# Inverse softmax sums as transposed rows, their transfers and the sum stores in ScalarE's stream, and the x norm in parts

## The chip, the cores and the metric

The kernel runs on one core of one Trainium2 chip. A core has five instruction streams, each worked off strictly in its order: PE (TensorE, matmuls), DVE (VectorE), ACT (ScalarE), POOL (GpSimd) and SP (SyncE, which here only issues transfers). A stream that waits for a semaphore holds everything behind it. A transfer (DMA) is issued by one of SP, ACT or POOL and runs on 16 DMA engines that all of them share; whoever needs its data waits for its semaphore. The metric is the device time of one execution in microseconds.

## The reference

One decoder block for 512 tokens of width 1024, in float32. The input is RMS-normed and projected to q, k, v and a gate z for two attention branches of 8 heads of 64, to two sigmoid gates, and to 8 forget logits:

```python
h = rms_norm(x, norm_g[layer])
proj = h @ w_in[layer]
fq, fk, fv, fz, mq, mk, mv, mz, ga, gb, fl = split_cols(proj, IN_SPLITS)
q = rms_norm(to_heads(fq, FOX_HEADS), fox_q_g[layer]); k = ...; v = to_heads(fv, FOX_HEADS)
log_f = log_sigmoid(fl + b_f[layer])
y_fox = from_heads(fox_attention(q, k, v, log_f)) * silu(fz)     # causal softmax with decay
q = partial_rope(rms_norm(to_heads(mq, MOBA_HEADS), moba_q_g[layer]), positions); k = ...
y_moba = from_heads(moba_attention(q, k, v)) * silu(mz)
merged = (sigmoid(ga + b_gate[layer, 0]) * (y_fox @ w_fox[layer])
          + sigmoid(gb + b_gate[layer, 1]) * (y_moba @ w_moba[layer]))
x = x + merged @ w_out[layer]
```

With 512 tokens and blocks of 256, the block-sparse branch selects every earlier block, so both branches are full causal softmax attention. Each softmax row is divided by its sum; this change is about how the inverses of these sums get to where they are used.

## The kernel before, in words

Tokens are cut into 4 tiles of 128, the width into 8 chunks `k` of 128. A float32 product is made of three matmuls with operands split into a high and a low part (`h`, `l`); `split` makes these parts for each weight chunk, on ACT and DVE. Weights come in pieces of 512 KB over SP's queue (`wr`).

The program is written as a list of units, but a planner orders each engine's stream by its own estimate of a timeline. So the order of the source is a wish; the stream order is what the planner made of it. Dependencies become semaphore waits in those streams.

The stages:

- Head. The first q and k projections run on unnormed input (`Z`, with the gain folded in). `x_stats` gives the inverse norm `r` per token. `normalise` broadcasts `r` over partitions (four PE transposes into `p_rbc`, a copy to `rbc`) and scales the eight chunks `XT[k]`, each one product on DVE, one copy to `Gh` on ACT, one subtraction to `Gl` on DVE. The gate units `fza` and `fzb` (`unit_z`, two each) multiply `Z` with weights, scale by `rbc` (`zs`) and apply SiLU. `forget` computes the log-sigmoid of the forget logits in about 30 small DVE operations and one exponential, its cumulated sum by matmul, and `LR` through `p_LR`.
- Attention, in four groups of four heads: fox a, fox b, moba a, moba b. In a group, `Tr(pr)` transposes q and k of a pair of heads (`p_qT`, `p_kT`); `Aa(h)` makes logits (`lg`), the masked maximum on DVE, the exponential with row sums `rsum` on ACT (L521); `Bb(h)` transposes the probabilities (`p_a`, `p_b`, `p_cc`), splits them (`pth`, `ptl`) and multiplies with v (`pv`); `Yp(pr)` multiplies the pair's output with z and the inverse sums and splits it (`yh`, `yl`). Between these pieces stand the projections of the next group as filler (`pj`): each evacuated unit of q or k goes through `norm_qk` (square on ACT, sum `ss` on DVE, power `ff` and product `qn` on POOL, L301 and L303) and, for moba, `do_rope` on POOL (L333 to L339). `Tr` of the next group waits for these `qn`.
- The inverse sums. After the second head of a pair, `inverse_sums` takes the reciprocal `ri` (`rinv`) of 128 partitions by 8 values, writes it to DRAM from POOL's queue as `r_dram` (L535), and reads each head's 512 values back, spread over 64 partitions, into `rinv_bc` (L537, two loads, also POOL's queue). `Yp` multiplies z into `rinv_bc` on POOL (L593; on DVE for the last pair) and DVE multiplies the result into `ypair` (L594).
- The activation sums. `make_sums(k)` forms four sums and differences of chunks of the normed input for the gates' fast block product, splits them, and stores them from POOL's queue to DRAM (L242, 16 stores of 256 KB); `load_sums` reads them at the start of the gates.
- Gates and output: block products `GA`, `GB`, the branch projections `wf`, `wm`, and `wo` with the residual.

PSUM has the pools `pj` (2 buffers), `tp` (3), `lg` (2) and `pv` (1). In `attn_group` three lists are returned: head, body and tail of a group; the main part interleaves body and tail with filler and the next group's head.

Of the kernel before, what the change touches and what calls it, by code (L numbers as in the profile page):

```python
# [29 lines left out]
def fox_moba_kernel(ctx: ExitStack, tc, xT, x, w_in, w_fl, w_fox, w_moba, w_out, cst, rope, out):  # L30
# [37 lines left out]
    def col(c, n=1):  # L68
        return cs[:, c:c + n]
# [137 lines left out]

    rbc = con.tile([P, S], F32, name="rbc")

    def normalise():  # L210

        p = pst("lg", 2, "p_rbc")
        for t in range(NT):
            T.transpose(p[:, t * P:(t + 1) * P], r[:, t:t + 1].to_broadcast([P, P]), ident)
        A.activation(rbc, p, AF.Copy)
        for k in range(KT):
            V.scalar_tensor_tensor(XT[k], XT[k], col(C_NG + k), rbc, op0=OP.mult, op1=OP.mult)
            A.activation(Gh[:, k, :], XT[k], AF.Copy)
            V.tensor_tensor(out=Gl[:, k, :], in0=XT[k], in1=Gh[:, k, :].bitcast(F32), op=OP.subtract)
# [8 lines left out]
    def make_sums(k):  # L228
        def tl(tag, dt=F32):
            return t2("y", 15, f"sum_{tag}", dt=dt)  # L230
        a, b = XT[k], XT[k + 4]
        f0, f1 = tl("sf"), tl("sf")
        s3, s2, s1, s4 = f0[:, 0:HT], f0[:, HT:S], f1[:, 0:HT], f1[:, HT:S]
        for o, x, y, op in ((s3, a[:, 0:HT], a[:, HT:S], OP.subtract), (s1, a[:, HT:S], b[:, HT:S], OP.add),
                            (s2, s1, a[:, 0:HT], OP.subtract), (s4, b[:, 0:HT], s2, OP.subtract)):
            V.tensor_tensor(out=o, in0=x, in1=y, op=op)
        for i, f in enumerate((f0, f1)):
            hl = [tl("sh", F32R), tl("sl", F32R)]
            A.activation(hl[0], f, AF.Copy)
            V.tensor_tensor(out=hl[1], in0=f, in1=hl[0].bitcast(F32), op=OP.subtract)  # L240
            for d, t in zip(S_dram, hl):
                nc.gpsimd.dma_start(out=d[2 * i:2 * i + 2, :, k, :].rearrange("s p t -> p s t"),  # L242
                                    in_=t.bitcast(F32).rearrange("p (s t) -> p s t", t=HT))

    def load_sums():
        for i in range(4):
# [130 lines left out]

    def unit_z(name, c):
        def go():
            p = pj(f"pz_{name}{c}")  # L380
            tr_mm(p, name, c)
            z = t2("y", 15, f"zs_{name}{c}")
            s = t2("u", 4, "sg")
            if name[0] == "f":
                V.tensor_tensor(out=z, in0=p, in1=rbc, op=OP.mult)
                A.activation(s, z, AF.Sigmoid)
                V.tensor_tensor(out=z, in0=z, in1=s, op=OP.mult)
            else:
# [10 lines left out]
    def zero_kl():  # L399
# [6 lines left out]
        for o in range(2):  # L406
            rows = slice(HD, P) if o == 0 else slice(0, HD)
            for tl in KLt[o] + [Q2t[o]]:
                G.memset(tl[rows, :].bitcast(F32), 0.0)

    def forget():
        n = NT * 8
        f2 = xf.rearrange("p t h -> p (t h)")

        def sm(nm, w=n):
            return stage["pool"].tile([P, w], F32, name=nm)
        na, e, d, s, s2, acc, lf = (sm(f"fg_{i}") for i in range(7))
        pre = stage["pool"].tile([P, NT, 8], F32, name="fg_pre")
        V.tensor_scalar(na, f2, -1.0, None, op0=OP.mult)
        V.tensor_tensor(out=na, in0=na, in1=f2, op=OP.min)  # L420
        A.activation(e, na, AF.Exp)
# [48 lines left out]
    def attn_group(br, half, gq, gk):  # L470
# [36 lines left out]
        def Aa(h):  # L507
            def go():
                qs, kh, kl, q2 = st[h]
                hh = hb + h  # L510
                pts = []
                for i in range(NT):
                    n = P * (i + 1)
                    lg = pst("lg", 2, "lg")
                    qt = slice(i * P, (i + 1) * P)
                    T.matmul(lg[:, :n], qs[:, qt], kh[:, :n], start=True, stop=False)  # L516
                    T.matmul(lg[:, :n], q2[:, qt], kl[:, :n], start=False, stop=True)  # L517
                    pt = stage["pool"].tile([P, n], F32, name=f"p{i}", tag=f"p{i}", bufs=2)
                    V.tensor_tensor_reduce(pt, lg[:, :n], mask[:, 512 - n:512], -0.125, 3.0e38,  # L519
                                           op0=OP.add, op1=OP.min, accum_out=mkn[:, hh, i:i + 1])  # L520
                    A.activation(pt, pt, AF.Exp, bias=mkn[:, hh, i:i + 1], scale=-1.0,  # L521
                                 accum_out=rs[:, hh, i:i + 1])
                    pts.append(pt)
                st[h] = pts
                if h % 2:
                    inverse_sums(h // 2)
            return go

        def inverse_sums(pr):


            h0 = hb + 2 * pr
            V.reciprocal(ri[:, h0:h0 + 2, :], rs[:, h0:h0 + 2, :])
            rb = st["r", pr] = stage["pool"].tile([P, S], F32, name="rinv_bc", tag="rinv_bc", bufs=1)
            G.dma_start(out=R_dram[h0:h0 + 2].rearrange("h t p -> p h t"), in_=ri[:, h0:h0 + 2, :])  # L535
            for o in range(2):
                G.dma_start(out=rb[o * HD:(o + 1) * HD, :],  # L537
                            in_=R_dram[h0 + o].rearrange("t p -> (t p)").partition_broadcast(HD))

        def Bb(h):  # L540
            def go():
# [39 lines left out]
                sh = t2("u", 4, "ysh")  # L581
                A.activation(sh[me, :], pv[ot, :], AF.Copy)  # L582
                V.tensor_tensor(out=y[me, :], in0=pv[me, :], in1=sh[me, :], op=OP.add)  # L583
            return go

        def Yp(pr):
# [10 lines left out]
                Y[br, gp] = (yh, yl)  # L597
            return go

        return ([Tr(0)], [Aa(0), Aa(1), Tr(1), Bb(0), Aa(2), Bb(1), Yp(0), Aa(3)], [Bb(2), Bb(3), Yp(1)])  # L600


    FS, MG = {}, {}
# [247 lines left out]
        evac_qk(b1[t], "fqa", t)  # L851
    for t in range(NT):
        evac_qk(b2[t], "fka", t)
    normalise()
    pump(0)
    fz = filler(["fza", "fzb"])
    for u in fz[:2]:
        u()
    forget()
    for u in fz[2:]:  # L860
        u()
    seq(["fva"])
    enter("attention")
    zero_kl()
# [5 lines left out]
    head, body, tail = attn_group("f", "a", col(C_FQ), col(C_FK))  # L870
    HALF[0] = False
    head[0]()
    for n in range(4):
        nxt = []
# [86 lines left out]
```

## Time and profile before

| what | us |
|---|---|
| median of three runs | 472.12 |
| their range | 471.99 to 472.58 |
| the profiled execution, as a run | 476.4 |
| its span, first to last instruction | 474.7 |
| PE busy | 435.7 (92%) |
| DVE busy | 311.9 (66%) |
| ACT busy | 262.0 (55%) |
| POOL busy | 115.6 (24%) |
| granted PE clock, mean | 0.959 |

All stretches and durations come from the one profiled execution. A row of the waits names engine, tile and line of the waiting instruction and then what ended the wait. A row of a timeline gives start and duration in us, engine, line, operation, what it writes and reads, shapes, and in brackets the idle time of the engine before it. A row of stretches gives the busy time of PE, PE's weight loads, DVE, ACT and POOL, then the granted clock of PE as a share of full speed. Issuing a transfer is not counted as busy on ACT, but is on POOL. Matmuls are pipelined, so neighbouring rows overlap.

### The profile page before, as it was taken

The page shows a single profiled execution, that of the slowest core. Times are in us where ns is not written, and L with a number is a line of the kernel's source. Part 1 is how long each engine was busy: PE and PEld are TensorE (multiplying, and loading weights), DVE is VectorE, ACT ScalarE, POOL GpSimd, SP SyncE. Part 2 cuts the span into 40 slices and gives each one's busy share as a digit, 9 for nine tenths or more (in the row PEclk, how much of TensorE's full clock was granted, in tenths as well). Part 3 has the DMA queues.
Part 4 walks back from the last instruction along what each step waited for, and adds up shares of the span by engine and source line. Part 5 has one row for each costly group of instructions (what it writes and reads, how often), then busy time and mean ns, then how long its engine had stood idle before and what let it go on. Part 6 is the DMA issues. An engine that isn't in the chain of part 4 may idle for free.

```text
span 474.7 us, 8105 instructions
## 1 busy us (share of the span) xinstructions
PE 435.7 (92%) x3092; PEld 408.9 (86%) x3092; DVE 311.9 (66%) x553; ACT 262.0 (55%) x489; POOL 115.6 (24%) x146
## 2 busy tenths in 40 slices
PE   7998999996999939999597989978999999999997
PEld 6996899995999937899596768868999989989996
DVE  5489997686368654578544588634889788664411
ACT  5877456784478633797423588633755645532200
POOL 4046058206338351103563001231000000000000
PEclk9999999998899977999889889997999999999999
DMA  8970478572442712411424130119331611652331
GB/s 257 379 252 11 133 236 269 147 115 58 78 134 46 62 51 63 116 57 26 129 59 110 35 100 0 24 34 402 120 103 76 206 61 62 204 178 83 121 111 44
DMA packets 22390, 56.39 MB, mean 119 GB/s; under 512 B 3472, under 2 KB 7696, under 8 KB 22352
## 3 DMA queue, kind: packets, MB, share of 16 engines
q1 hardware_dynamic: 14240, 39.98, 28.8%
q0 software_dynamic: 3456, 10.52, 7.5%
q10 hardware_dynamic: 4656, 5.38, 4.3%
q8 instruction: 24, 0.39, 0.4%
q14 instruction: 14, 0.11, 0.1%
HBM read 46.27 MB, written 6.32 MB: 111 GB/s over the span
## 4 chain that ended last, share of the span: by engine, by line
PE 58%; DMA 21%; DVE 6%; POOL 6%; ACT 5%; issue 3%; POOLq 0%; DVEq 0%; ACTq 0%
DMA r_dram<-rinv 8%; DMA rinv_bc<-r_dram 6%; PE pb_GB L681 3%; PE pb_GB L684 3%; PE pb_GB L683 3%; PE pb_GA L681 3%; PE pb_GA L684 3%; PE pb_GA L683 3%; PE po L781 2%; PE po L783 2%; PE po L782 2%; POOL ff L301 2%; DMA wr_fka<-in_w_in_dram 2%; DMA x<-in_x_dram 2%; DMA KH<-KH 2%
## 5 line engine op out<-in xcount | busy, mean ns | idle before, releaser
L521 ACT ACTIVATE p<-p,negm 128x128 f32<-128x128 f32 (+1 forms) x64 | 35.6, 557 | 7.5 <-DVE negm L519 7.2
L519 DVE CUSTOM_DVE_ANT_0 p<-lg,mask 128x128 f32<-128x128 f32 (+1 forms) x64 | 30.2, 483 | 13.3 <-PE lg L517 12.8
L301 POOL TENSOR_TENSOR ff<-ss,mh 128x8 f32<-128x8 f32 x16 | 28.7, 1800 | 21.3 <-DVE ss L299 20.6
L781 PE MATMUL po<-wh_wo,mgh 128*128 128x256 f32 x96 | 27.1, 282 | 0.0
L783 PE MATMUL po<-wh_wo,mgl 128*128 128x256 f32 x96 | 27.1, 282 | 0.0
L782 PE MATMUL po<-wl_wo,mgh 128*128 128x256 f32 x96 | 27.0, 281 | 0.0
L537 POOL DMA_DIRECT2D rinv_bc<-r_dram x16 | 8.6, 540 | 65.0 <-DMA r_dram<-rinv 56.0
L791 DVE TENSOR_TENSOR ot<-po,xr 128x256 f32<-128x256 f32 x16 | 6.6, 425 | 24.8 <-PE po L783 23.6
L112 DVE TENSOR_TENSOR wl_GA<-wr_ga,wh_GA 128x1024 fp32r<-128x1024 f32 x14 | 16.9, 1221 | 8.8 <-ACT wh_GA L110 5.8
L516 PE MATMUL lg<-KH,QS 128*128 128x128 f32 (+1 forms) x64 | 21.4, 341 | 0.7 <-DMA KH<-KH 0.4
L494 DVE SCALAR_TENSOR_TENSOR KL<-p_kT,cs,KH 64x512 fp32r<-64x512 f32 x16 | 12.0, 749 | 15.2 <-ACT KH L492 14.8
L110 ACT ACTIVATE wh_wo<-wr_wo 128x1024 fp32r<-128x1024 f32 x8 | 8.5, 1061 | 21.6 <-PE po L783 8.0
L110 ACT ACTIVATE wh_GA<-wr_ga 128x1024 fp32r<-128x1024 f32 x14 | 14.6, 1059 | 10.3 <-PE pb_GA L683 4.4
L582 ACT ACTIVATE ysh<-pv 64x512 f32<-64x512 f32 x16 | 9.5, 594 | 18.3 <-PE pv L558 18.1
L112 DVE TENSOR_TENSOR wl_GB<-wr_gb,wh_GB 128x1024 fp32r<-128x1024 f32 x14 | 16.8, 1222 | 4.2 <-ACT wh_GB L110 3.3
L110 ACT ACTIVATE wh_GB<-wr_gb 128x1024 fp32r<-128x1024 f32 x14 | 14.6, 1058 | 8.5 <-PE pm L611 2.5
L781 PEld LDWEIGHTS po<-wh_wo,mgh 128*128 128x128 f32 x96 | 18.1, 189 | 0.0
L782 PEld LDWEIGHTS po<-wl_wo,mgh 128*128 128x128 f32 x96 | 18.1, 189 | 0.0
L783 PEld LDWEIGHTS po<-wh_wo,mgl 128*128 128x128 f32 x96 | 18.1, 188 | 0.0
L492 ACT ACTIVATE KH<-p_kT,cs 64x512 fp32r<-64x512 f32 x16 | 10.8, 678 | 13.0 <-PE p_kT L482 12.8
L535 POOL DMA_DIRECT2D r_dram<-rinv x8 | 7.7, 957 | 38.1 <-DVE negm L519 33.6
L583 DVE TENSOR_TENSOR ypair<-pv,ysh 64x512 f32<-64x512 f32 x16 | 11.0, 688 | 8.8 <-ACT ysh L582 8.6
(449 smaller groups left out, 1843.8 us busy)
## 6 DMA issues: line engine op xcount, KB each, us to landing
wr_ga<-in_w_in_dram SPq DMA_DIRECT2D x8, 512.0 KB, 4.1
wr_gb<-in_w_in_dram SPq DMA_DIRECT2D x8, 512.0 KB, 5.1
wr_wo<-in_w_out_dram SPq DMA_DIRECT2D x8, 512.0 KB
xt<-in_xT_dram SPq DMA_DIRECT2D x8, 256.0 KB
x<-in_x_dram SPq DMA_DIRECT2D x8, 256.0 KB, 7.7
s_dramh<-sum_sh POOLq DMA_DIRECT2D x8, 256.0 KB, 3.8
s_draml<-sum_sl POOLq DMA_DIRECT2D x8, 256.0 KB, 4.5
KH<-KH ACTq DMA_DIRECT2D x16, 128.0 KB, 3.0
```

The costliest lines, as they stand in the source:

```text
L110: A.activation(hi[:, :, 0:n], src, AF.Copy)
L112: eng.tensor_tensor(out=lo[:, q, 0:n], in0=src[:, q], in1=hi[:, q, 0:n].bitcast(F32), op=OP.subtract)
L301: G.tensor_tensor(out=f2, in0=ss.rearrange("p t h -> p (t h)"), in1=mh, op=OP.pow)
L516: T.matmul(lg[:, :n], qs[:, qt], kh[:, :n], start=True, stop=False)
L519: V.tensor_tensor_reduce(pt, lg[:, :n], mask[:, 512 - n:512], -0.125, 3.0e38, op0=OP.add, op1=OP.min, accum_out=mkn[:, hh, i:i + 1])
L521: A.activation(pt, pt, AF.Exp, bias=mkn[:, hh, i:i + 1], scale=-1.0, accum_out=rs[:, hh, i:i + 1])
L681: T.matmul(o, hi[:, k, cc], lh, start=(n < 3 and c == 0 and k == 0), stop=False, skip_group_check=True)
L683: T.matmul(o, hi[:, k, cc], ll, start=False, stop=False, skip_group_check=True)
L684: T.matmul(o, lo[:, k, cc], lh, start=False, stop=(k == 3), skip_group_check=True)
L781: T.matmul(p[:, :CW], gh[:, st], hi[:, k, :CW], start=(kk == 0), stop=False)
L782: T.matmul(p[:, :CW], gh[:, st], lo[:, k, :CW], start=False, stop=False)
L783: T.matmul(p[:, :CW], gl[:, st], hi[:, k, :CW], start=False, stop=(kk == KT - 1))
```

## The change

Four things change.

The inverse sums. `inverse_sums` keeps only the reciprocal. `sums_out`, at the end of `Bb` of a pair's first head, has PE transpose the 128 by 8 values to 8 by 128 in a `tp` buffer, ACT copy them to `rinv_t`, and ACT's queue store the eight rows to `r_dram`. `sums_in` issues the two loads of `rinv_bc` from ACT's queue: for a group's first pair after `Aa(2)`, for the second after `Bb(3)`.

The sum stores. `make_sums` returns a function that issues its four stores from ACT's queue, called after the unit that follows. The sums move from the units of `fqb` and `fkb` to those of `fvb` and `mqa`.

The head. `norm_row` makes `rbc`; `normalise` takes some of the chunks, and the three parts (0 to 2, 3 to 5, 6 and 7) stand behind the first three gate units. `forget_exp` (the argument and the exponential) comes ahead of it, the rest of `forget` behind all four gate units. `fzb` uses `tp` buffers for its products instead of `pj`.

The gate of a group's second pair. `Yp(1)` leaves the tail; it stands behind the first piece of the next group's body, and in the last group between the two units of `wf3`.

```diff
-    def normalise():
-
+
+    def norm_row():
         p = pst("lg", 2, "p_rbc")
         for t in range(NT):
             T.transpose(p[:, t * P:(t + 1) * P], r[:, t:t + 1].to_broadcast([P, P]), ident)
         A.activation(rbc, p, AF.Copy)
-        for k in range(KT):
+
+    def normalise(*ks):
+        for k in ks:
             V.scalar_tensor_tensor(XT[k], XT[k], col(C_NG + k), rbc, op0=OP.mult, op1=OP.mult)
...
-            for d, t in zip(S_dram, hl):
-                nc.gpsimd.dma_start(out=d[2 * i:2 * i + 2, :, k, :].rearrange("s p t -> p s t"),
-                                    in_=t.bitcast(F32).rearrange("p (s t) -> p s t", t=HT))
+            out.extend((d[2 * i:2 * i + 2, :, k, :].rearrange("s p t -> p s t"),
+                        t.bitcast(F32).rearrange("p (s t) -> p s t", t=HT)) for d, t in zip(S_dram, hl))
+
+        def store():
+            for d, t in out:
+                A.dma_start(out=d, in_=t)
+        return store
...
-            p = pj(f"pz_{name}{c}")
+            p = (tp if name == "fzb" else pj)(f"pz_{name}{c}")
...
+    def forget_exp():
+        f2 = xf.rearrange("p t h -> p (t h)")
+        FG.extend(stage["pool"].tile([P, NT * 8], F32, name=f"fg_{i}") for i in range(7))
+        na, e = FG[:2]
+        V.tensor_scalar(na, f2, -1.0, None, op0=OP.mult)
+        V.tensor_tensor(out=na, in0=na, in1=f2, op=OP.min)
+        A.activation(e, na, AF.Exp)
...
                 if h % 2:
                     inverse_sums(h // 2)
+                elif h:
+                    sums_in(0)
             return go
 
         def inverse_sums(pr):
             h0 = hb + 2 * pr
             V.reciprocal(ri[:, h0:h0 + 2, :], rs[:, h0:h0 + 2, :])
+
+        def sums_out(pr):
+            h0 = hb + 2 * pr
+            p = tp("p_ri")
+            T.transpose(p[:8, :P], ri[:, h0:h0 + 2, :].rearrange("p h t -> p (h t)"), ident)
+            rt = sb.tile([8, P], F32, name="rinv_t", tag="rinv_t", bufs=1)
+            A.activation(rt, p[:8, :P], AF.Copy)
+            A.dma_start(out=R_dram[h0:h0 + 2].rearrange("h t p -> (h t) p"), in_=rt)
+
+        def sums_in(pr):
             rb = st["r", pr] = stage["pool"].tile([P, S], F32, name="rinv_bc", tag="rinv_bc", bufs=1)
-            G.dma_start(out=R_dram[h0:h0 + 2].rearrange("h t p -> p h t"), in_=ri[:, h0:h0 + 2, :])
             for o in range(2):
-                G.dma_start(out=rb[o * HD:(o + 1) * HD, :],
-                            in_=R_dram[h0 + o].rearrange("t p -> (t p)").partition_broadcast(HD))
+                A.dma_start(out=rb[o * HD:(o + 1) * HD, :],
+                            in_=R_dram[hb + 2 * pr + o].rearrange("t p -> (t p)").partition_broadcast(HD))
...
                 V.tensor_tensor(out=y[me, :], in0=pv[me, :], in1=sh[me, :], op=OP.add)
+                if o == 0:
+                    sums_out(pr)
+                elif pr:
+                    sums_in(1)
             return go
...
-        return ([Tr(0)], [Aa(0), Aa(1), Tr(1), Bb(0), Aa(2), Bb(1), Yp(0), Aa(3)], [Bb(2), Bb(3), Yp(1)])
+        return ([Tr(0)], [Aa(0), Aa(1), Tr(1), Bb(0), Aa(2), Bb(1), Yp(0), Aa(3)], [Bb(2), Bb(3)], [Yp(1)])
...
-    normalise()
+    forget_exp()
+    norm_row()
     pump(0)
     fz = filler(["fza", "fzb"])
-    for u in fz[:2]:
+    for k, u in enumerate(fz):
         u()
+        if k < 3:
+            normalise(*range(3 * k, min(3 * k + 3, 8)))
     forget()
-    for u in fz[2:]:
-        u()
...
-                def with_sums(u=fill[2 * k], k=k):
+                store = []
+
+                def with_sums(u=fill[2 * k + 8], k=k, store=store):
                     u()
-                    make_sums(k)
-                fill[2 * k] = with_sums
+                    store.append(make_sums(k))
+
+                def with_store(u=fill[2 * k + 8 + 1], store=store):
+                    u()
+                    store[0]()
+                fill[2 * k + 8], fill[2 * k + 8 + 1] = with_sums, with_store
         inter(body + ([following] if n < 3 else []) + tail, fill)
         if n < 3:
-            body, tail = nxt[1:]
+            body, tail = nxt[1][:1] + gate + nxt[1][1:], nxt[2]
+            gate = nxt[3]
+    wf3 = filler(["wf3"])
+    wf3[0]()
+    gate[0]()
+    wf3[1]()
     enter("gates")
     load_sums()
-    seq(["wf3", "GA0", "GA1", "GB0", "wm0", "wm2", "GB1"])
+    seq(["GA0", "GA1", "GB0", "wm0", "wm2", "GB1"])
```

More of the change, by code (lines that the diff above doesn't have):

```diff
@@ L231, in make_sums @@
         a, b = XT[k], XT[k + 4]
+        out = []
         f0, f1 = tl("sf"), tl("sf")
@@ L409, in zero_kl @@
                 G.memset(tl[rows, :].bitcast(F32), 0.0)
+    FG = []
+    def forget_exp():
[5 more added lines that the diff above has]
+        A.activation(e, na, AF.Exp)
     def forget():
@@ L413, in forget @@
         f2 = xf.rearrange("p t h -> p (t h)")
-        def sm(nm, w=n):
-            return stage["pool"].tile([P, w], F32, name=nm)
-        na, e, d, s, s2, acc, lf = (sm(f"fg_{i}") for i in range(7))
+        na, e, d, s, s2, acc, lf = FG
         pre = stage["pool"].tile([P, NT, 8], F32, name="fg_pre")
-        V.tensor_scalar(na, f2, -1.0, None, op0=OP.mult)
-        V.tensor_tensor(out=na, in0=na, in1=f2, op=OP.min)
-        A.activation(e, na, AF.Exp)
         V.tensor_scalar(d, e, 2.0, None, op0=OP.add)
@@ L869, in fox_moba_kernel @@
             ("m", "b", C_MQ, C_MK, ["mzb", "wf0", "wf1", "wf2"]))
-    head, body, tail = attn_group("f", "a", col(C_FQ), col(C_FK))
-    HALF[0] = False
+    head, body, tail, gate = attn_group("f", "a", col(C_FQ), col(C_FK))
     head[0]()
```

## The prediction

> **What bounds the kernel now.** I read the waits of the matmul engine (PE) first, then what its releasers did in that time, then the granted clock behind each wait. The waits of PE, longest first (engine, line, releaser: total us, times, longest us):
>
> ```profile
> PE p_kT L482 <- POOL qn_mka L339: 8.1, 1, 8.1
> PE p_qT L480 <- POOL qn_mqb L339: 5.6, 1, 5.6
> PE pv L558 <- DVE ptl L554: 4.9, 1, 4.9
> PE p_kT L482 <- POOL qn_mkb L339: 4.6, 1, 4.6
> PE p_kT L482 <- POOL qn_fkb L303: 4.5, 1, 4.5
> PE pz_fzb L372 <- DVE fg L426: 2.3, 1, 2.3
> ```
>
> Four gaps end when POOL has normalised a q or k tile, one when DVE has made `ptl`, one in the head of the kernel. Together they are 30.0 us. The reader is to see that no throughput explains them: each is one long wait. The timeline of POOL shows what it did before (start, duration, instruction, idle time before it and its releaser):
>
> ```profile
> 108.57 1.08 POOL L537 DMA_DIRECT2D rinv_bc<-r_dram  x2 [9.01 <-issue]
> ...
> 164.10 1.09 POOL L537 DMA_DIRECT2D rinv_bc<-r_dram  x2 [6.70 <-DMA r_dram<-rinv]
> ...
> 171.07 1.26 POOL L593 TENSOR_TENSOR rinv_bc<-zs_fzb,rinv_bc 128x512 f32<-128x512 f32 x1 [5.32 <-DMA rinv_bc<-r_dram]
> ...
> 177.91 0.44 POOL L339 TENSOR_TENSOR qn_mka<-ra,rb 128x128 f32<-128x128 f32 x1
> ...
> 224.25 1.09 POOL L537 DMA_DIRECT2D rinv_bc<-r_dram  x2 [8.07 <-DMA r_dram<-rinv]
> ...
> 253.14 1.10 POOL L537 DMA_DIRECT2D rinv_bc<-r_dram  x2 [7.31 <-DMA r_dram<-rinv]
> ```
>
> POOL stands still for 6.7 to 9.0 us until the inverse sums have landed in DRAM, issues the two loads that spread them over partitions, and stands still again until these land (5.32 us at 171.07). Only then it goes on to `qn_mka`, whose last step ends at 178.35, where the 8.1 us gap ends. The fifth gap is the same chain on DVE, which does the multiplication L593 of the last pair itself, with `ptl` behind it in its stream:
>
> ```profile
> 321.22 0.69 DVE L593 TENSOR_TENSOR rinv_bc<-zs_mzb,rinv_bc 128x512 f32<-128x512 f32 x1 [8.49 <-DMA rinv_bc<-r_dram]
> ```
>
> A gap costs more than its length. Stretches with busy times and, after POOL, the granted clock: first the work right behind the five long gaps, then the short gap in the head.
>
> ```profile
> 117.51:121.90 4.39, 4.39 (x21) 4.39 (x22) 1.51 (x3) 1.82 (x3) 3.96 (x3) 0.50 0.46 120
> 178.40:183.30 4.90, 4.90 (x19) 4.51 (x20) 2.88 (x4) 3.78 (x6) 0.87 (x1) 0.50 0.49 125
> 237.90:241.30 3.40, 3.39 (x16) 3.39 (x17) 2.58 (x4) 1.99 (x5) 3.32 (x2) 0.50 0.41 117
> 262.14:265.20 3.06, 3.06 (x9) 2.49 (x10) 1.55 (x3) 2.05 (x3) 0.00 (x0) 0.50 0.15 33
> 322.60:326.70 4.10, 4.10 (x19) 4.10 (x20) 2.44 (x3) 0.80 (x2) 0.00 (x0) 0.50 1.02 410
> ```
> ```profile
> 42.00:44.30 2.30, 0.01 (x2) 0.04 (x1) 2.30 (x5) 2.15 (x4) 1.00 (x1) 1.00 0.00 0
> ```
>
> After each long gap PE works 3.1 to 4.9 us at a granted clock of 0.50, 19.85 us together. At full clock that is half the time: 9.9 us lost beside the gaps. So 27.7 (five gaps) + 9.9 + 2.3 = 39.9 us hang on the waits that this change touches. In the 246 us of attention the engines stand thus:
>
> ```profile
> 80.00:326.00 246.00, 215.74 (x1455) 199.57 (x1454) 157.39 (x318) 151.06 (x318) 81.50 (x99) 0.93 0.35 82
> ```
>
> PE is busy 216, DVE 157, ACT 151, POOL 82 us: ACT, which takes the transfers over, has 95 us free, and 61 if some 34 us go from the stretch.
>
> **The change part by part.** What lands how fast (KB each, median us from issue to landing), and what ACT's and PE's pieces cost:
>
> ```profile
> KH<-KH ACTq DMA_DIRECT2D x16, 128.0 KB, 3.0
> rinv_bc<-r_dram POOLq DMA_DIRECT2D x16, 128.0 KB, 5.3
> ...
> out_dram<-ot ACTq DMA_DIRECT2D x16, 128.0 KB, 2.3
> ...
> r_dram<-rinv POOLq DMA_DIRECT2D x8, 4.0 KB, 9.5
> ```
> ```profile
> L521 ACT ACTIVATE p<-p,negm 128x128 f32<-128x128 f32 (+1 forms) x64 | 35.6, 557 | 7.5 <-DVE negm L519 7.2
> L110 ACT ACTIVATE wh_GA<-wr_ga 128x1024 fp32r<-128x1024 f32 x14 | 14.6, 1059 | 10.3 <-PE pb_GA L683 4.4 <-PE pf L611 3.1 <-issue 2.8
> L553 ACT ACTIVATE pth<-p_a 128x512 fp32r<-128x512 f32 x16 | 9.5, 593 | 4.1 <-PE p_a L547 4.0
> L521 ACT ACT_TABLE_LOAD x4 | 5.1, 1283 | 0.1
> ```
> ```profile
> 76.27 0.60 PE L454 MATMUL p_LR<-ident,c 128*64 128x128 f32 x4
> 76.71 0.60 PE L480 MATMUL p_qT<-ident,qn_fqa 128*128 128x128 f32 x4
> 77.15 0.60 PE L482 MATMUL p_kT<-ident,qn_fka 128*128 128x128 f32 x4
> ```
>
> Rows instead of single values: `r_dram<-rinv` moves 4 KB as 1024 separate floats and takes 9.5 us. After the change it is eight rows of 128 floats from ACT's queue. The trace has no such small row transfer; the nearest row is `out_dram<-ot`, also ACT's queue into DRAM, 2.3 us at 128 KB. Ends: 2.3, and 9.5 if it is the write to DRAM and not the form that costs. I take 2.3 to 3.0 (`KH<-KH`, same queue). Added ahead of it are the PE transpose, a copy and a hand-over, under 1 us. The chain to the multiplication is then shorter by 9.5 − 3.5 = 6.0 us.
>
> POOL's stream: all 8 stores and 16 loads of the inverse sums and the 16 stores of the activation sums leave it. POOL keeps its wait for `rinv_bc`, ahead of the q and k norms as before. Take 6.0 us off each gap: 8.1 leaves 2.1; 5.6, 4.6, 4.5 and 4.9 leave nothing. The order of the streams is planned anew, and in the changed order POOL has the whole `mkb` chain behind one such wait, so I leave 3.0 of 27.7 (ends 0 and 12, half of each gap but the largest, rounded up): −24.7.
>
> The clock: with one gap of 2 to 3 us left instead of five over 4.4, I leave 1.0 of 9.9 (end: 4): −8.9. [...]
>
> Norm in parts: `fzb` takes its accumulators from another pool (`tp`, three buffers) and no longer waits for DVE, which had eight `xt` products and eight `Gl` subtractions ahead. DVE's total stays, and the log-sigmoid chain moves behind the gate units; its user, `p_LR`, comes at 76 us. −2.0 of 2.3 (ends 0 and −2.3).
>
> PE: eight more transposes; four of `p_qT` take 77.15 − 76.71 = 0.44 us of its stream, so 8 × 0.11 = +0.9. They borrow a `tp` buffer until ACT has copied it; cover is the other two.
>
> ACT gets 40 more DMA issues. One takes 0.47 us, but in the sequencer, while the engine still works off what it had:
>
> ```profile
> 87.97 0.67 ACT L492 ACTIVATE KH<-p_kT,cs 64x512 fp32r<-64x512 f32 x1
> 88.14 0.47 ACTq L503 DMA_DIRECT2D Q<-QS  x1
> 88.54 0.61 ACT L521 ACTIVATE p<-p,negm 128x384 f32<-128x384 f32 x1
> ```
>
> That is 18.8 us of issue, mostly covered. Eight small copies, at most 0.4 each: 3. In the changed order the gate's sigmoids of the last group stand apart: two more table loads, 2.6. And a new wait: the first load of each pair waits in ACT's stream until the store has landed, and every softmax exponential, PSUM copy and weight split queues behind it. In the changed order the instructions between store and load are, by the durations above: one of 0.6 us (four pairs), 1.5 (one pair), and 2.2 to 2.7 (three pairs), 11.1 us in all. With a landing of 2.3 the uncovered rest is 4 × 1.7 + 0.8 + 0.1 = 7.7 us; with 3.0 it is 12.9. ACT's extra is thus 18.8 + 3 + 2.6 + 7.7 = 32 us against 61 free. PE waits for little of it, since its stream holds projection matmuls that ask nothing of ACT. I charge half of the uncovered waits, +4.0 (ends 0, and 32 if nothing is covered). The sum stores also wait on ACT for DVE's low halves, inside these ends.
>
> Sum against the profiled span: 474.7 − 24.7 − 8.9 − 2.0 + 0.9 + 4.0 = 444.0. That execution took 476.4 as a run, the median of the runs is 472.12, which is 2.6 under its span. Predicted: 444.0 − 2.6 = 441 us, 6.5% faster.
>
> **The rivals.**
>
> ACT binds beside PE. In the changed order 12 of the 16 sum stores stand in ACT's stream within the second group of heads, beside its own work. For: its extra 32 us come in half the span's time and its stream is in order. Against: 61 us free. If half of the 32 reaches PE instead of 4: 441 + 12 = 453 us.
>
> Everything fits: no gap left, no charge for ACT (−3 −1 −4): 433 us. For: the planner now orders around transfers that are short. Against: POOL's waits for `rinv_bc`, 5.3 us, stay.
>
> The other side: the store is slow because it writes DRAM, not because of its form. Then ACT instead of POOL stands still, 8 × 9.5 − 11.1 = 65 us. With all of it passed on to PE the sum is 441 − 4 + 65 = 502 us. It decides from a landing L where 8L − 11.1 exceeds the gain without ACT's charge, 35 us: L = 5.8 us, for all eight pairs. Against: 2.3 us of `out_dram`, with 32 times the bytes. [...]
>
> The change does not do what it says: the new plan puts the q and k chains as late again relative to PE, with POOL's own work (from the end of L593 at 172.33 to `qn_mka` at 178.35 a norm and rope chain takes 6.0 us) as the bound. Then gaps of the old size stay, less the clock and the head: about 470 us, equal within 0.5%.
>
> **How the numbers follow.** Forecast, 434 to 450 (ends: residual gaps 0 to 5, ACT 0 to 8): 0.60. ACT beside PE, 450 to 462: 0.18. Everything fits, under 434: 0.13. ACT blocked, over 473: 0.06. Plan as late as before: 0.03, split between the three signs. The range that leaves out about 2 in 10 is 430 to 459. Faster by over 0.2% (about what a measurement of this kernel can tell from no change) 0.92, same 0.01, slower 0.07.
>
> **What would show it.** Right: POOL has no wait for `r_dram`; its landing is under 3.5 us; the waits of PE on `qn` tiles are under 3 us each; clock 0.98 or more over the span; ACT shows waits of 1 to 2 us at the loads of `rinv_bc`. Wrong: `r_dram` landing above 5 us, or ACT idle before PSUM copies with PE waiting for ACT; a gap at `p_kT` over 4 us with the clock at 0.50 behind it; the stretch from first to last softmax over 225 us.

## The result, and the profile after

| what | before | after |
|---|---|---|
| median, us (four runs each, one chip) | 472.27 | 444.25 |
| range, us | 471.99 to 472.58 | 442.54 to 445.73 |
| profiled execution as a run, us | 476.4 | 445.57 |
| its span, us | 474.7 | 443.8 |
| granted PE clock, mean | 0.959 | 0.992 |

The ratio is 0.9405, with a 95% interval of 0.9361 to 0.945: 28.0 us less. The forecast was 441, inside a range of 430 to 459.

The busy line of the page after:

```profile
PE 430.1 (97%) x3100; PEld 405.3 (91%) x3100; DVE 310.7 (70%) x553; ACT 266.7 (60%) x499; POOL 88.5 (20%) x106
```

The span fell by 30.9 us. PE's busy time fell by 435.7 − 430.1 = 5.6 and its idle time by the other 25.3. The waits of PE after the change, longest first, without those at the program's start and end:

```profile
PE pb_GA L709 <- ACT e_GA L719: 2.5, 1, 2.5
PE pf L638 <- ACT f L652: 1.7, 2, 1.2
...
PE pv L580 <- ACT pth L576: 1.2, 2, 0.8
PE pv L581 <- DVE ptl L577: 0.6, 1, 0.6
```

No wait on any `qn` tile is left: the four gaps of 4.5 to 8.1 us behind POOL are gone, not merely shorter. Of what is left, the three longest end with ACT. POOL still waits in front of its gate multiplication, for the load of `rinv_bc` (this row counts four of these waits), but no longer for the store of the sums:

```profile
POOL rinv_bc L620 <- DMA rinv_bc<-r_dram: 23.9, 4, 17.0
```

The chain that ended last shows how long a store and a load take now (start, duration, what):

```profile
177.97 2.41 DMA r_dram<-rinv_t
...
289.66 6.55 DMA rinv_bc<-r_dram
```

2.41 us for this store, where the median had been 9.5. But the last load of `rinv_bc` takes 6.55 us, where the median had been 5.3. The timelines of ACT and then of DVE around that load, and a stretch (columns as in the prediction: busy PE, its weight loads, DVE, ACT, POOL, then clock, DMA share, GB/s):

```profile
289.13 0.45 ACTq L560 DMA_DIRECT2D rinv_bc<-r_dram  x1
...
289.66 0.58 ACTq L560 DMA_DIRECT2D rinv_bc<-r_dram  x1
...
298.47 0.63 ACT L622 ACTIVATE yhm<-ypair 128x512 fp32r<-128x512 f32 x1 [6.39 <-DVE ypair L621]
```
```profile
296.30 0.69 DVE L620 TENSOR_TENSOR rinv_bc<-zs_mzb,rinv_bc 128x512 f32<-128x512 f32 x1 [5.29 <-DMA rinv_bc<-r_dram]
```
```profile
289.00:296.30 7.30, 6.25 (x50) 5.91 (x49) 1.57 (x3) 1.39 (x3) 0.91 (x2) 1.00 0.95 297
```

The DMA engines are 95% busy, with the activation sums that the gates read and with weights. DVE waits 5.29 us for `rinv_bc`, ACT 6.39 us for DVE, and the copy `e_GA` that PE needs stands behind it in ACT's stream. That is the 2.5 us gap, now the largest.

The clock. First the two stretches that ran at half clock, then, in the same order, the stretch of 3.41 us ahead of each:

```profile
262.21:265.62 3.41, 3.41 (x10) 2.67 (x9) 3.38 (x9) 1.96 (x7) 0.00 (x0) 0.50 0.18 38
299.75:303.17 3.42, 3.42 (x17) 3.42 (x18) 2.65 (x4) 2.21 (x3) 0.00 (x0) 0.50 0.06 16
258.79:262.21 3.42, 1.77 (x8) 1.14 (x8) 2.49 (x4) 3.34 (x6) 0.00 (x0) 1.00 0.00 0
296.34:299.75 3.41, 0.90 (x8) 0.70 (x7) 2.65 (x4) 1.28 (x3) 0.00 (x0) 1.00 0.06 22
```

Two such stretches are left, 6.8 us of work at half clock or 3.4 us lost. Of those in the profile of before, the first and the fifth of six, with the sum of all six:

```profile
115.08:121.91 6.83, 4.40 (x21) 4.41 (x22) 3.92 (x7) 1.82 (x3) 6.31 (x5) 0.50 0.30 77
...
278.92:282.34 3.42, 3.31 (x13) 2.47 (x11) 3.36 (x12) 3.31 (x9) 0.00 (x0) 0.50 0.05 13
...
sum 37.56, PE 23.40 PEld 21.61 DVE 25.43 ACT 17.01 POOL 20.51; mean PE 3.90 PEld 3.60 DVE 4.24 ACT 2.83 POOL 3.42
```

23.4 us of work at half clock, 11.7 lost. The gain from the clock is thus 11.7 − 3.4 = 8.3 us between these two profiles. In a second profile of the changed kernel, `after_again` below, only the later of the two stretches is at half clock.

### The profile page after: what moved, and what is told of

Same layout as the page of the kernel before. It is cut to its first block, busy times and chain, and to the rows that moved or that the text cites. A ratio compares the mean times of both kernels' runs of the same rounds, so it can differ in the third digit from the quotient of the medians.

```text
span 443.8 us, 8080 instructions
## 1 busy us (share of the span) xinstructions
PE 430.1 (97%) x3100; PEld 405.3 (91%) x3100; DVE 310.7 (70%) x553; ACT 266.7 (60%) x499; POOL 88.5 (20%) x106
## 4 chain that ended last, share of the span: by engine, by line
PE 82%; DVE 6%; DMA 5%; ACT 5%; issue 1%; ACTq 0%; SPq 0%; DVEq 0%
PE pb_GB L709 3%; PE pb_GB L711 3%; PE pb_GB L712 3%; PE pb_GA L709 3%; PE pb_GA L712 3%; PE pb_GA L711 3%; PE po L809 3%; PE po L811 3%; PE po L810 3%; PE pv L581 2%; PE pv L580 2%; PE lg L527 2%; PE lg L528 2%; PE pm L638 2%; PE pm L639 2%; PE pm L640 2%
## 5 line engine op out<-in xcount | busy, mean ns | idle before, releaser
L308 POOL TENSOR_TENSOR ff<-ss,mh 128x8 f32<-128x8 f32 x16 | 27.6, 1726 | 78.6 <-DVE ss L306 76.4
L819 DVE TENSOR_TENSOR ot<-po,xr 128x256 f32<-128x256 f32 x16 | 6.6, 424 | 24.8 <-PE po L811 23.6
L501 DVE SCALAR_TENSOR_TENSOR QS<-p_qT,cs,QS 64x512 fp32r<-64x512 f32 x16 | 12.0, 750 | 7.1 <-ACT QS L500 6.7
L577 DVE TENSOR_TENSOR ptl<-p_a,pth 128x512 fp32r<-128x512 f32 x16 | 11.0, 688 | 5.9 <-ACT pth L576 5.8
L638 PE MATMUL pf<-yhf,wh_wf 128*128 128x512 f32 x32 | 13.4, 419 | 1.7 <-ACT f L652 1.7
L112 DVE TENSOR_TENSOR wl_wo<-wr_wo,wh_wo 128x1024 fp32r<-128x1024 f32 x8 | 9.8, 1222 | 7.4 <-ACT wh_wo L110 7.4
```

Of the source, the lines that this page charges most:

```text
L112: eng.tensor_tensor(out=lo[:, q, 0:n], in0=src[:, q], in1=hi[:, q, 0:n].bitcast(F32), op=OP.subtract)
L308: G.tensor_tensor(out=f2, in0=ss.rearrange("p t h -> p (t h)"), in1=mh, op=OP.pow)
```

## The experiments

The runs fall into three groups, each on a chip of its own. The kernel before took 476.69, 473.46 and 477.18 us in them, so times are compared within a group.

**First group: form or queue?** The theory: the store was slow because it wrote 1024 single floats, and rows cure that wherever they are issued. The first rival: it is ScalarE's queue that helps.

`rows_pool`, the changed kernel with the row store and its loads from GpSimd's queue:

```diff
-            A.dma_start(out=R_dram[h0:h0 + 2].rearrange("h t p -> (h t) p"), in_=rt)
+            G.dma_start(out=R_dram[h0:h0 + 2].rearrange("h t p -> (h t) p"), in_=rt)
...
-                A.dma_start(out=rb[o * HD:(o + 1) * HD, :],
+                G.dma_start(out=rb[o * HD:(o + 1) * HD, :],
```

> The changed kernel with the row store and the two loads of the inverse sums issued from POOL's queue again; transpose, copy and everything else as changed. Theory 'form': what cost was the landing of 1024 single floats, 9.5 us, whichever stream waits for it. Then POOL waits 2 to 3 us per pair where it waited 7 to 9, no wait of PE on a qn tile is over 3 us, and the time is 442 to 450 us. Rival 'queue': what cures is that POOL's stream has no wait between store and load at all. Then the q and k norms are late again, PE waits 4 us and more for qn tiles with the clock at 0.50 behind them, and the time is 455 to 470 us.

Measured: 442.44 us, ratio 0.9255 (0.919 to 0.9319). Landing of the transfers, then POOL's waits:

```profile
rinv_bc<-r_dram POOLq DMA_DIRECT2D x16, 128.0 KB, 3.2
...
r_dram<-rinv_t POOLq DMA_DIRECT2D x8, 4.0 KB, 2.3
```
```profile
POOL rinv_bc L620 <- DMA rinv_bc<-r_dram: 13.4, 5, 4.5
POOL rinv_bc L560 <- DMA r_dram<-rinv_t: 11.5, 6, 3.4
```

From the same queue that had needed 9.5 us, the rows land in 2.3. POOL waits again for store and load, 1.9 and 2.7 us on average and 4.5 at most, and PE waits for no `qn` tile. So the form did it, in this order of streams.

`before_rows`, the other way round: the kernel before, with the transpose alone.

```diff
-            G.dma_start(out=R_dram[h0:h0 + 2].rearrange("h t p -> p h t"), in_=ri[:, h0:h0 + 2, :])
+            p = tp("p_ri")
+            T.transpose(p[:8, :P], ri[:, h0:h0 + 2, :].rearrange("p h t -> p (h t)"), ident)
+            rt = sb.tile([8, P], F32, name="rinv_t", tag="rinv_t", bufs=1)
+            A.activation(rt, p[:8, :P], AF.Copy)
+            G.dma_start(out=R_dram[h0:h0 + 2].rearrange("h t p -> (h t) p"), in_=rt)
```

> The kernel before with the transpose alone: PE turns the inverse sums, ACT copies them, POOL's queue stores eight rows and loads them as before, at the same place in the source. Theory 'form': POOL's wait for the store falls from 7 to 9 us to 2 to 3, the four gaps of PE on qn tiles and the one on ptl go, with the clock loss behind them: 440 to 450 us. Rival 'queue': POOL's stream still holds both waits ahead of the norms, gaps stay at 3 us and more: 455 to 470 us.

Measured: 453.12 us, ratio 0.9468 (0.9393 to 0.9544): 23.6 us less than the kernel before, by this one edit. Its page lists the landing, and its waits of PE are headed by a new one:

```profile
r_dram<-rinv_t POOLq DMA_DIRECT2D x8, 4.0 KB, 1.7
```
```profile
PE p_ri L536 <- DVE rinv L533: 4.1, 2, 3.2
PE pv L561 <- DVE ypair L587: 2.5, 1, 2.5
```

Here the transpose stands right behind the reciprocal, and PE waits for it. In the changed kernel it comes at the end of the next `Bb`, and that wait is not there. So the place of the transpose matters, too. The time lies between the two expected bands: no wait on `qn` or `ptl` tiles of the old length is left, as the form would have it, but these new waits and one of 1.9 us for `KH` take a part of the gain back.

`floats_act`, the changed kernel without the transpose: 1024 floats, issued from ScalarE's queue.

```diff
-            p = tp("p_ri")
-            T.transpose(p[:8, :P], ri[:, h0:h0 + 2, :].rearrange("p h t -> p (h t)"), ident)
-            rt = sb.tile([8, P], F32, name="rinv_t", tag="rinv_t", bufs=1)
-            A.activation(rt, p[:8, :P], AF.Copy)
-            A.dma_start(out=R_dram[h0:h0 + 2].rearrange("h t p -> (h t) p"), in_=rt)
+            A.dma_start(out=R_dram[h0:h0 + 2].rearrange("h t p -> p h t"), in_=ri[:, h0:h0 + 2, :])
```

> The changed kernel without the transpose: the 128 by 8 inverse sums are stored float by float from ACT's queue, at the same place, and loaded from ACT's queue. Theory 'form': the store lands after 9 to 10 us as it did from POOL's queue, ACT stands still some 8 us at each of eight pairs, about 65 us in all, and most of it reaches PE: 480 to 510 us, slower than the kernel before. Rival 'queue': POOL's stream is free, ACT's wait is covered by PE's projections: 444 to 455 us.

Measured: 508.8 us, ratio 1.0643 (1.0559 to 1.0727), slower than the kernel before. The waits of ACT, then those of PE:

```profile
ACT qn_fkb L287 <- issue: 11.2, 1, 11.2
...
ACT ysh L601 <- issue: 9.5, 1, 9.5
```
```profile
PE lg L527 <- DMA KH<-KH: 18.5, 2, 12.4
PE pv L576 <- ACT pth L572: 10.8, 4, 4.8
PE pv L576 <- DVE ypair L602: 9.3, 1, 9.3
PE pj_fvb L280 <- ACT qn_fkb L287: 6.8, 1, 6.8
```

In such waits ACT stands still for 7.4 to 11.2 us at a time. The view names no releaser, but the timeline places them: at all eight pairs the first load is issued 9.1 to 12.5 us behind its store, and the late instruction stands right behind that load. PE waits with it: for PSUM copies, and for the transfers of `KH` that ACT issued late. This is the rival "the other side" as I had priced it (502 us), with the slow store put back by hand. So the change is a pair: the move into ScalarE's stream is affordable only because the rows are fast.

`norm_whole`, the changed kernel with the head of before (norm in one piece, `fzb` in `pj`):

```diff
-    forget_exp()
     norm_row()
+    normalise(*range(KT))
     pump(0)
...
-    for k, u in enumerate(fz):
+    for u in fz[:2]:
         u()
-        if k < 3:
-            normalise(*range(3 * k, min(3 * k + 3, 8)))
+    forget_exp()
     forget()
+    for u in fz[2:]:
+        u()
```

> The changed kernel with the head of the kernel before: norm of x in one piece, log-sigmoid between the gate units, fzb in pj buffers. By the prediction's step for the norm in parts the gap of 2.3 us before pz_fzb is back and the time is about 2 us over the changed kernel's: 446 to 447 us. Rival: the gap comes back but is made up for by the projections after it, which DVE's lateness does not hold: within 0.5 us of the changed kernel.

Measured: 445.13 us, the median of four runs from 443.31 to 453.13. The ratio, 0.9305 (0.9224 to 0.9385), leaves out the longest run, which is the profiled one. No changed kernel ran beside it, so it prices nothing. Its profile shows one thing, in stretches cut at the edges of its half-clock stretch:

```profile
42.20:45.61 3.41, 1.29 (x6) 0.71 (x4) 3.41 (x4) 3.11 (x6) 2.41 (x2) 1.00 0.00 0
45.61:49.02 3.41, 3.12 (x7) 2.48 (x8) 3.41 (x7) 2.14 (x3) 0.00 (x0) 0.50 0.00 0
```

The same gap that left the clock at 1.00 in the kernel before (42.00 to 44.30) halves it here, in this one execution: its mean clock is 0.977, and 0.992 to 0.999 in the other three runs. I come back to this below.

**Second group: which parts are worth what?** The changed kernel again, and three variants.

> The changed kernel as it stands, beside the variants on one chip, so that small differences between them can be read. Its ratio to the kernel before was 0.9405 on its own chip; the theories have no quarrel here: about 0.935 to 0.945. The gap of 2.5 us ahead of the first gate product (at 297 us) and the half clock behind it should come again, since neither depends on chance.

> The row store of the inverse sums and its loads from GpSimd's queue, all else as changed. Theory 'form' (the rows take the store's time away, the queue is free to choose): within 0.3% of the changed kernel on this chip, thus within 1.5 us either way. Rival 'queue' (ScalarE's stream is worth something by itself, since GpSimd's waits of up to 17 us for the store are gone from it): 1% or more slower than the changed kernel, 4.5 us and up. A third possibility from the first run on another chip (ratio 0.9255 against 0.9405): the move to ScalarE's stream cost something, and this kernel is 0.4% or more faster, 2 us and up.

`gate_tail`, the changed kernel with `Yp(1)` back in the tail and `wf3` whole behind attention:

```diff
-        return ([Tr(0)], [Aa(0), Aa(1), Tr(1), Bb(0), Aa(2), Bb(1), Yp(0), Aa(3)], [Bb(2), Bb(3)], [Yp(1)])
+        return ([Tr(0)], [Aa(0), Aa(1), Tr(1), Bb(0), Aa(2), Bb(1), Yp(0), Aa(3)], [Bb(2), Bb(3), Yp(1)])
...
-            body, tail = nxt[1][:1] + gate + nxt[1][1:], nxt[2]
-            gate = nxt[3]
-    wf3 = filler(["wf3"])
-    wf3[0]()
-    gate[0]()
-    wf3[1]()
+            body, tail = nxt[1:]
...
-    seq(["GA0", "GA1", "GB0", "wm0", "wm2", "GB1"])
+    seq(["wf3", "GA0", "GA1", "GB0", "wm0", "wm2", "GB1"])
```

> The changed kernel with the gate of the second pair back in the group's tail, ahead of the next group's first logits, and wf3 back as a whole behind attention; the stores and loads as changed. Theory 'place' (the move of the gate keeps DVE and ScalarE, which would wait for the last loads, from holding up the next group's first blocks): waits of PE on lg or pv at the group starts of 1 to 2 us each, 3 to 6 us in all with the clock behind them, ratio about 0.95. Rival 'form alone' (with rows, the loads land before the gate needs them, and where it stands is all one): within 1.5 us of the changed kernel.

`sums_pool`, the changed kernel with the stores of the activation sums from GpSimd's queue:

```diff
-                A.dma_start(out=d, in_=t)
+                G.dma_start(out=d, in_=t)
```

> The changed kernel with the 16 stores of the activation sums issued from GpSimd's queue and not from ScalarE's. I predicted the stores' issue at about no cost on ScalarE (half of a microsecond each, beside PE). Theory 'no cost either way': within 1 us of the changed kernel. Rival 'ScalarE's stream is late by their issue' (16 x 0.4 to 0.75 us in the first group, where ScalarE feeds PE): this kernel 3 to 6 us faster. Rival 'GpSimd is late' (its waits for the sums hold up the norms of q and k behind them, as before): waits of PE on qn tiles come back, 2 us or more slower.

| kernel | median, us | range of six runs, us | ratio, 95% interval |
|---|---|---|---|
| `after_again` | 444.01 | 441.1 to 447.01 | 0.9366 (0.9326 to 0.9407) |
| `rows_pool_again` | 440.03 | 439.62 to 441.35 | 0.9295 (0.9268 to 0.9323) |
| `gate_tail` | 438.75 | 437.19 to 440.67 | 0.9266 (0.9235 to 0.9297) |
| `sums_pool` | 445.29 | 443.28 to 448.57 | 0.9406 (0.9367 to 0.9446) |

Two of my theories fell. I had expected waits at the group starts with the gate in the tail and a ratio of about 0.95, but it is 5.3 us faster than the changed kernel. And the row transfers from GpSimd's queue are 4.0 us faster, the third possibility named. Why is open: in the profile of `rows_pool_again` PE even waits 4.0 us ahead of `pb_GA`, for the load of `S0h`, and only waits of 2.0 us and less are gone. The sum stores are worth nothing either way that these runs resolve (1.3 us between overlapping intervals).

Why the gate's old place is better: the gap of 2.5 us ahead of `pb_GA` is not among the waits of `gate_tail`. Its ACT timeline at the same loads:

```profile
282.22 1.11 ACTq L560 DMA_DIRECT2D rinv_bc<-r_dram  x2
```

They stand ahead of the bulk transfers of the next stage there. Its last loads of activation sums (`S3h`, `S3l`) are issued at 284.5 and 285.0 and its next weights `wr_ga` from 287.7. In the changed kernel these come at 288.8, 289.4 and 285.6, so that the last load of `rinv_bc`, at 289.7, is behind them all. In `gate_tail` the load takes 3.1 us, with the DMA engines 70% busy from 281 to 290 us, against 6.55. DVE still waits 3.5 us for it, but PE has `wf` units to do. A second wait goes as well: `pf` for ACT's `f`, 1.7 to 1.9 us, stands in all seven profiles of kernels with the gate moved and in none of the five with the gate in the tail. The repeated profile of the changed kernel has the gap ahead of `pb_GA` again (2.45 us, half clock behind it) and, over all gaps of more than 0.3 us, 11.1 us of PE idle against 5.1. The move of the gate was a loss inside the gain.

**Third group: do the two add up, what is the head worth, and what halves the clock?**

> The gate of the second pair in the tail, beside the next three on one chip. First run: 1.2% under the changed kernel (ratio 0.9266 against 0.9366). If that was the place of the gate and not chance, the ratio is 0.924 to 0.930 again; if it was chance, nearer to 0.937.

`gate_pool` joins the edits of `gate_tail` and `rows_pool`.

> The gate in the tail and the row store and loads from GpSimd's queue at once. Each alone was 0.7 to 1.2% under the changed kernel. Theory 'one and the same place' (both repair the wait for the last loads, which sits ahead of the first gate product): they don't add up, the ratio is within 0.3% of the kernel with the gate in the tail. Rival 'two costs': 2 to 4 us less than it, ratio about 0.92.

`gate_norm_whole` joins those of `gate_tail` and `norm_whole`.

> The gate in the tail, and the head as before: the norm in one piece, fzb's products in the pool pj. It prices the split norm by itself. My sum had 2.0 us for it, the gap alone, with no clock behind a gap of 2.3 us. Rival from the traces since (the clock halves after a window of 3.41 us in which PE stood idle for more than about half): gap of 2.3 to 2.4 plus 1.7 for the clock behind it if the gap falls into one such window, about 4 us; 2.4 if it is cut by a window's edge.

| kernel | median, us | range of six runs, us | ratio, 95% interval |
|---|---|---|---|
| `gate_tail_again` | 438.93 | 438.24 to 440.07 | 0.9191 (0.9159 to 0.9223) |
| `gate_pool` | 448.52 | 446.57 to 449.59 | 0.9391 (0.9353 to 0.943) |
| `gate_norm_whole` | 442.4 | 440.45 to 442.94 | 0.9257 (0.9224 to 0.9291) |

`gate_tail` repeats its time to 0.2 us. Its ratio does not repeat: 0.9191 is below the expected 0.924 to 0.930, since the kernel before was 3.7 us slower on this chip. No run of the changed kernel stands beside it here. The head's 3.5 us lie between the two expectations for `gate_norm_whole`, 2.4 and about 4. Neither theory for `gate_pool` held: the two edits don't add up and aren't one, they harm each other, by 9.6 us. The waits of PE in `gate_pool`, its POOL timeline ahead of the second of these, and then POOL of `gate_tail_again` at the same gate:

```profile
PE lg L527 <- DMA KH<-KH: 3.4, 1, 3.4
PE p_kT L493 <- POOL qn_mka L346: 3.0, 1, 3.0
PE p_qT L491 <- POOL qn_mqb L346: 1.7, 1, 1.7
```
```profile
155.62 1.13 POOL L560 DMA_DIRECT2D rinv_bc<-r_dram  x2 [1.35 <-DMA r_dram<-rinv_t]
159.41 1.29 POOL L620 TENSOR_TENSOR rinv_bc<-zs_fzb,rinv_bc 128x512 f32<-128x512 f32 x1 [2.66 <-DMA rinv_bc<-r_dram]
...
166.41 1.17 POOL L346 TENSOR_TENSOR qn_mka<-ra,rb 128x128 f32<-128x128 f32 x1
```
```profile
154.77 1.29 POOL L620 TENSOR_TENSOR rinv_bc<-zs_fzb,rinv_bc 128x512 f32<-128x512 f32 x1 [0.39 <-DMA rinv_bc<-r_dram]
```

The second and third are the old chain in small: POOL stands 1.35 us for the store and 2.66 for the load, ahead of the gate and the norms of `mka` behind it, and PE waits for `qn_mka`. From ScalarE's queue the load has landed but for 0.39 us when POOL gets there (1.34 in the first profile of `gate_tail`). What makes `KH` late, for the longest of the three waits, these rows do not show. So ScalarE's queue is the better one where the gate stands ahead of the next norms, and GpSimd's, by 4.0 us, where it has been moved behind the next group's first piece. My first verdict on the queue held for one order of the streams only.

The head by itself is 442.4 − 438.93 = 3.5 us. The new place of the activation sums, and `fzb`'s buffers apart from the norm in parts, were in no run by themselves.

`stalls`, `gate_tail` with four waits of PE put among the last output units:

```diff
+    STALL = {(1, 2): 1, (2, 1): 3, (3, 0): 4, (3, 3): 6}
+    LAST = [None]
...
             p = pj(f"po{n}{t}")
             st = slice(t * P, (t + 1) * P)
+            g0 = MG[0][0][:, CW * (t // 2):CW * (t // 2) + CW]
+            for _ in range(STALL.get((n, t), 0)):
+                V.scalar_tensor_tensor(g0, LAST[0][:, :CW], 0.0, g0.bitcast(F32), op0=OP.mult, op1=OP.add)
+            LAST[0] = p
```

> The kernel with the gate in the tail, with four waits of PE added among the last twelve output units, where it otherwise has none: DVE rewrites a left operand in place (one, three, four and six products of 128 by 256, times zero plus itself), and PE can't go on before. Estimated from DVE's rows: gaps of about 1.1, 1.9, 2.3 and 3.2 us, each with two units or more of dense work behind it. [...] Rule 'share of a window' (the clock changes only on a grid of 3.41 us, and a window that is idle for over half halves the next one): the gap of 1.1 never does, those of 1.9 and 2.3 do if over 1.7 us of them fall into one window, that of 3.2 does if it isn't cut in the middle; each halving adds about 1.7 us.

Measured: 454.47 us in a single run, span 452.8. The waits of PE, then stretches in pairs on the grid on which the clock changes, the one with the gap and the one behind it:

```profile
PE po L816 <- DVE mgh L809: 8.1, 4, 3.1
```
```profile
405.50:408.92 3.42, 2.57 (x22) 2.37 (x21) 1.44 (x3) 0.00 (x0) 0.00 (x0) 1.00 0.31 95
408.92:412.33 3.41, 3.41 (x31) 3.41 (x30) 0.42 (x1) 0.00 (x0) 0.00 (x0) 1.00 0.29 81
415.74:419.16 3.42, 1.65 (x14) 1.45 (x14) 2.60 (x5) 0.00 (x0) 0.00 (x0) 1.00 0.36 104
419.16:422.57 3.41, 3.41 (x18) 3.41 (x18) 0.00 (x0) 0.00 (x0) 0.00 (x0) 0.50 0.15 50
429.40:432.81 3.41, 1.29 (x11) 1.32 (x12) 1.87 (x5) 0.00 (x0) 0.00 (x0) 1.00 0.29 77
432.81:436.22 3.41, 3.41 (x19) 3.41 (x18) 0.24 (x1) 0.00 (x0) 0.00 (x0) 0.50 0.02 5
443.05:446.46 3.41, 1.47 (x12) 1.48 (x13) 1.74 (x5) 0.00 (x0) 0.00 (x0) 1.00 0.11 38
446.46:449.88 3.42, 2.86 (x14) 2.56 (x13) 0.42 (x1) 0.00 (x0) 0.00 (x0) 0.50 0.00 0
```

PE is idle 0.85, 1.77, 2.12 and 1.94 us in the four stretches. Behind the first the clock stays at 1.00, behind the others it is 0.50. PE worked for 1.29 us or more of each of the four, so a stretch need not be idle as a whole to have one at half clock behind it.

## Why the prediction was right, point by point

**The form of the store.** Taken: a landing of 2.3 to 3.0 us. Measured: 2.41 on the chain after, 2.3 and 1.7 from GpSimd's queue. That single floats were the cause, and not the write to DRAM, is shown from both sides by `before_rows` (23.6 us gained) and `floats_act` (32.1 lost), each against the kernel before.

**The five gaps, 27.7 with 3.0 left.** Right in size by luck, wrong about which would be left. The four behind POOL left nothing. The fifth, which I had written down to nothing, stayed as DVE's wait of 5.29 us; behind it now stands ACT's copy and not `ptl`, and PE loses 2.5 us there. Two things failed there. I let the last pair's load take what the others do, and it took 6.55 us, issued behind the sums' and the weights' transfers. And the sum has no term for the gate's move, which put the load there: in `gate_tail` it takes 3.1 us and PE's gap is gone.

**The clock, −8.9.** Measured −8.3 (11.7 to 3.4), so the size is near. The 1.0 us that I left for one gap of 2 to 3 us was my estimate, and no run shows it: in the changed kernel 3.4 us were lost in two stretches. My own trace also spoke against putting the loss down to the long gaps alone. The row at 278.92 above is at half clock, though in the 3.41 us ahead of it PE was idle for only 1.28, in gaps of 0.73 at most; my 19.85 us left it out. I let the gap at 42 us cost its own length only, since the clock over it was 1.00. That gap was cut by an edge of the grid. The stretches of the kernel before, cut on its own grid:

```profile
40.02:43.43 3.41, 1.98 (x9) 1.28 (x7) 3.41 (x3) 3.11 (x6) 2.98 (x3) 1.00 0.00 0
43.43:46.84 3.41, 2.55 (x11) 2.15 (x12) 3.41 (x7) 2.71 (x4) 0.00 (x0) 1.00 0.00 0
```

Idle 1.43 of 3.41 and then 0.86, both under half. In `norm_whole` 2.12 us of it fell into one stretch, and the next one ran at half. In `gate_norm_whole` 1.69 us did, just under half, and the next one stayed at 1.00.

**Norm in parts, −2.0.** Measured 3.5 us, by `gate_norm_whole`. The mechanism was right (the wait of `pz_fzb` on DVE's `fg` returns, 1.7 us in that profile), the size too small. What the clock adds to it in some executions I had left out; how much of the 1.5 us more is that, these runs do not say.

**PE, +0.9.** PE's busy time fell by 5.6 us where the clock alone gives 8.3, so the added work would be 2.7. But the second profile of the same kernel (PE busy 426.3, 1.7 of it lost to the clock) gives 0.6 by the same sum, so one pair of profiles cannot settle this term. The row of the eight transposes (shortest, median and longest in ns):

```profile
L552 PE MATMUL p_ri<-ident,rinv x8: 270/270/272, 97.9 to 285.5; 128*8 128x128 f32 x8
```

They take 8 × 0.27 = 2.2 us if nothing of them overlaps, where I had costed one at 0.11. How much does overlap is not settled.

**ACT's waits, +4.0.** PE waits for ACT 2.5 + 1.7 + 1.2 = 5.4 us after. Before, it waited 1.1:

```profile
PE p_a L547 <- ACT p L521: 1.1, 2, 0.7
```

Right in size, but by luck. 2.5 and 1.7 of it came with the gate's move and are not there in `gate_tail`, and I had no term for that. What I did charge for, ACT held at the loads until a store has landed, shows clearly only once. Ahead of the load at 237.53 us a semaphore wait in ACT's stream took 1.43 us, to 2.39 us behind the issue of its store; those in the 2.6 us ahead of the other pairs' loads took 0.04 and less. Beside the loads of the other seven pairs ACT is idle for 0.9 us or less at a time, whatever ended it, but for 1.47 behind the last one, which PE's `pv` ended. My sum had 1.7 us uncovered at each of four pairs, and 7.7 in all; how much of PE's last 1.2 us goes back to such waits is not shown. The sum stores on ACT cost nothing that the runs resolve, as costed.

**The sum and the offset.** The span came out at 443.8 against 444.0. That is closer than its terms: PE's idle time fell by 25.3 where the terms give 24.7 + 2.0 − 4.0 = 22.7, and its busy time by 5.6 where they give 8.0. The misses cancel. Nearly the whole error of 3.25 us is the last step: I took 2.6 off for the median, since the profiled execution of before ran that much above it. The profile after did not: its span lies 0.45 below the median.

**The rivals.** "ACT binds beside PE" (453) did not come. "The other side" (502) came when the slow store was put back, 508.8. "Everything fits" (433) did not come, but `gate_tail` went about half of the way there from the changed kernel, by undoing a part of the change: the change would have been worth 34.7 us on that chip without its move of the gate, 29.5 with it. The plan "as late as before" (470) did not come: no `qn` wait is left. Of the signs I had named, POOL's wait for `r_dram`, the landing, the `qn` waits and the clock came as told. Of ACT's waits of 1 to 2 us at the loads there is one. The stretch from the first to the last softmax is 198.7 us; my bound of 225 told nothing, since it was 220.1 before.

## What to carry to other kernels

Count the separate pieces of a small transfer, not only its bytes: here 4 KB as 1024 floats took 9.5 us, as eight rows 1.7 to 2.4, and a PE transpose of 0.27 us and a copy of 0.27 bought that. When a chain gets shorter, move its neighbours one at a time: here the gate's move, made together with it, gave back 5.3 us, and the choice of queue was worth 9.6 us or −4.0 depending on where the gate stood. A load that is needed at a stage's end is to be issued ahead of the bulk transfers of the next stage: here it took 3.1 us ahead of them and 6.55 behind.

## What the runs showed of the hardware

**The granted clock changed on a grid of 3.41 us.** In all 14 profiles the changes of the granted clock lie 3.41 us apart or a multiple of it; in the kernel before, for one, at 115.08, 121.91, 173.11 and 183.35 us, which is 2, 15 and 3 times 3.41. I cut each profile on its own grid and took PE's idle time in each stretch from its instructions. Of the stretches at full clock, all 30 with 57% idle or more are followed by one at half clock, none of those with 36% or less, and 9 of the 21 between. Of those at half clock, all 20 with 22% idle or more were followed by another, and none of the 38 with 9% or less. These are counts from these traces; what decides the clock inside the chip they do not show. From them I estimate that a gap of 2 to 3.4 us costs up to 1.7 us more, half of a stretch, where it falls into one stretch, and may cost nothing more where an edge cuts it.

**ScalarE's queue and its engine.** The issues cost little: moving 16 of them to GpSimd's queue changed the time by 1.3 us, which the runs do not resolve. A wait ahead of an issue held the whole stream: 7.4 to 11.2 us at a time in `floats_act`, about as long as the slow store of 9.5.

**The same load took twice as long at the wrong moment.** With the rows, `rinv_bc` lands in 3.0 to 3.2 us by the medians of `rows_pool`, `before_rows` and `gate_pool`, and the last one of the changed kernel took 6.55 with the DMA engines 95% busy. No run changes their load alone. In the kernel before the median is 5.3 us; why, no run shows.
